# Rotating the MLA queries on GpSimd alone, spreading the w_up sums over 18 items, and moving the low-rank scaling and the key rotation back

## The chip, the cores and the metric

The kernel runs on one core of a Trainium2 chip. The metric is the time of one execution in microseconds (us). TensorE is written PE (its weight loads PEld), VectorE DVE, ScalarE ACT, GpSimd POOL; SP is the engine whose queue issues most of the transfers.

## The reference, cut to what matters

The program is a two-layer encoder trunk on 1024 tokens of width 1024, in float32. Each layer has a mixer with three head groups, a cross-attention to 256 memory tokens, and a gated feed-forward network. The change touches the mixer's latent attention (MLA) and one preparation of the feed-forward network. What is computed there:

```python
qa = (rms_norm(c_q, mla_q_norm) @ mla_w_uq).reshape(B, S, 6, 64 + 32)
q_nope, q_pe = qa[..., :64], apply_rope(qa[..., 64:], *rope_a)
kva = (rms_norm(c_kv, mla_kv_norm) @ mla_w_ukv).reshape(B, S, 6, 64 + 64)
k_pe = apply_rope(k_rope.reshape(B, S, 1, 32), *rope_a)    # one key part for all six heads

def apply_rope(x, cos, sin):                               # pairs (a, b) of neighbouring elements
    return a * cos - b * sin, a * sin + b * cos
```

Six GQA heads stand beside the six MLA heads. Each head's scores are a 1024 x 1024 matrix, its softmax is taken by rows, and the result multiplies the values.

## The kernel before

Float32 operands are split into a high and a low part of a type that PE multiplies fast: `split` (L121 to L127) lets ACT write the high part and DVE the low one (lines L123 and L124, or L126 and L127 with a scale), and `mm3` (L116 to L118) makes a product from three matmuls. Weights go through `load`: a transfer, a high part by ACT (L108) or POOL (L110), and a low part by DVE (L111).

The mixer first multiplies the normalised input by the columns of `w_in` in stages; the last stage gives the low-rank query `cq` (two tiles, one for each half of the tokens), the low-rank key and value `ckv`, and the 32 rotary key columns `kr`. At the last token tile of each half, the code computes the root mean squares (L551 and L552 on DVE, a power on POOL in L553) and scales `cq` and `ckv` on DVE (L556, two instructions). After the stage `rope` rotates `kr`: four products and two sums, of which POOL makes two products (L237, L239) and DVE the rest (L236, L238, L240, L241).

Then `attention` runs 24 items, one for each head and half of the queries: items 0 to 11 are GQA, 12 to 23 MLA. An item has four steps of 128 query rows. A step multiplies queries and keys into a pair of PSUM banks (L726 and L727 for GQA, `mm3` for MLA); DVE finds the row maximum (L295), ACT the exponential with its sum (L299), DVE the reciprocal (L304), and POOL scales the row (L305). PE transposes the scaled rows (L140), which needs all four steps of the item, and multiplies them by the values (L318, L319); POOL adds the two halves of the result (L328). The four steps of an item are called scale 0 to scale 3 below, by their L305; scale 3 is the one that the transposes wait for last.

Between these steps stands other work, taken from `fill[i]`, the list of functions of item i: the transposes of `cq` and the up-projection of the queries (`turn_cq`, `q_cols`) in items 0 to 3, the rotation of each MLA head's queries (`rope_q(h)` in item 8 + 2h, with the same `rope`), the sum of squares of the outputs (L664), and more. `extra[i]` holds the transfers of item i. They prepare block sums of the weight `w_up`: 24 times `copy` copies a piece in DRAM by a transfer of SP (L778), and `add` adds another piece to it by an accumulating transfer that POOL issues (L783); an add waits until its copy has landed. Steps n = 0 to 23 are copied in item n * 14 // 24 and added four items later. The same list holds 12 copies for `w_down`, over 20 items.

Tiles are taken from 46 slots. A scheduler orders the instructions of each engine when the program is built, by its own estimate of when each is ready, so instructions can stand earlier in an engine's order than in the code; each engine then works in that order.

Of the kernel before, what the change touches and what calls it, by code (L numbers as in the profile page):

```python
# [8 lines left out]
F32 = mybir.dt.float32  # L9
F32R = mybir.dt.float32r  # L10
AF = mybir.ActivationFunctionType
ALU = mybir.AluOpType
AX = mybir.AxisListType

P = 128
D = 1024
S = 1024
NT = S // P
KT = D // P
CH = 512  # L20
NC = S // CH
TPC = CH // P
DEPTH = 2
EPS = 1e-6
GRID_W = 64
ROPE_THETA = 10000.0
MLA_H, NOPE, ROPE, QK_A = 6, 64, 32, 96
# [42 lines left out]
def trunk(ctx: ExitStack, tc: tile.TileContext, a: dict, out: bass.AP):  # L70
    nc = tc.nc
# [7 lines left out]
    sl = Slots(spool, SLOTS)  # L79
# [7 lines left out]
    def stat():  # L87
        return stats.tile([P, 16], F32, tag="stat", name="stat")
# [7 lines left out]
    def v3(ap, b):  # L96
        return ap.rearrange("p (a b) -> p a b", b=b)
# [134 lines left out]
    def rope(z, cos, sin, tmp):  # L232

        ev, od = z[..., 0], z[..., 1]
        t0, t1, t2, t3 = tmp
        nc.vector.tensor_tensor(t0, ev, cos, ALU.mult)  # L236
        nc.gpsimd.tensor_tensor(t1, od, sin, ALU.mult)  # L237
        nc.vector.tensor_tensor(t2, ev, sin, ALU.mult)  # L238
        nc.gpsimd.tensor_tensor(t3, od, cos, ALU.mult)  # L239
        nc.vector.tensor_tensor(ev, t0, t1, ALU.subtract)  # L240
        nc.vector.tensor_tensor(od, t2, t3, ALU.add)  # L241
# [142 lines left out]
    def layer(l, nt, w_m, last):  # L384
# [129 lines left out]
        def turn_q(j, c):  # L514
# [7 lines left out]
            if c == 1:  # L522
                sl.put(zq[j])

        cq = [sl.get(F32) for _ in range(2)]
        ckv = sl.get(F32)
        kr = lpool.tile([P, NT * ROPE], F32, tag="kr", name="kr")
        for t in range(NT):
# [17 lines left out]
            if t == 6:  # L546
                turn_q(0, 0)
                turn_q(0, 1)
            if tt == TPC - 1:
                v, r = stat(), stat()  # L550
                nc.vector.tensor_scalar(v[:, 0:4], ssq[:, 0:4], 1.0 / 256, EPS, ALU.mult, ALU.add)  # L551
                nc.vector.tensor_scalar(v[:, 4:8], ssq[:, 4:8], 1.0 / P, EPS, ALU.mult, ALU.add)  # L552
                nc.gpsimd.tensor_tensor(r[:, :8], v[:, :8], mhalf[:, :8], ALU.pow)  # L553
                for z, n, o in ((cq[c], 256, 0), (ckv[:, c * CH : (c + 1) * CH], P, 4)):
                    z = v3(z, n)
                    nc.vector.tensor_tensor(z, z, r[:, o : o + 4].unsqueeze(2).to_broadcast([P, TPC, n]), ALU.mult)  # L556
        put2(w_a)
# [3 lines left out]
        cos3, sin3 = v3(tab[:, T_COSA : T_COSA + P], 16), v3(tab[:, T_SINA : T_SINA + P], 16)  # L561
        tmp = sl.get(F32)
        rope(kr.rearrange("p (t i two) -> p t i two", i=16, two=2), cos3, sin3, [v3(tmp[:, o * P : (o + 1) * P], 16) for o in range(4)])
        sl.put(tmp)

# [41 lines left out]

        def rope_q(h):
            tmp = sl.get(F32)
            z = v3(qn[h][:, : NT * QK_A], QK_A)[:, :, NOPE:]  # L610
            rope(z.rearrange("p t (i two) -> p t i two", two=2), cos3, sin3, [v3(tmp[:, o * P : (o + 1) * P], 16) for o in range(4)])
            sl.put(tmp)
            if h == MLA_H - 1:
                sl.put(tab)

# [183 lines left out]
        items += [mla(h, c) for h in range(MLA_H) for c in range(NC)]  # L799
        fill[0] += [lambda k=k: turn_cq(0, k) for k in range(2)]  # L800
        fill[1] += [lambda k=k: turn_cq(1, k) for k in range(2)]
# [7 lines left out]
        for h in range(MLA_H):  # L809
            fill[8 + 2 * h] += [lambda h=h: rope_q(h)]  # L810
        fill[7] += [lambda c=c: turn_kr(c) for c in range(NC)]
# [40 lines left out]
        for n, (w, m, i) in enumerate(steps):  # L852
            g = n * 14 // len(steps)
            extra.setdefault(g, []).append(lambda w=w, m=m, i=i: w.copy(m, i))
            extra.setdefault(g + 4, []).append(lambda w=w, m=m, i=i: w.add(m, i))
        later = deque(sorted(w_d.steps(), key=lambda s: (5, 7, 6, 3).index(s[1])))
# [626 lines left out]
```

## Time and profile before

| | us |
|---|---|
| median of 3 runs | 2800.31 (2798.71 to 2804.17) |
| the profiled execution | 2792.72 |
| its span, first to last instruction | 2790.7 |
| PE busy in it | 2732.1 (98%) |
| DVE busy | 1966.8 (70%) |
| ACT busy | 1469.7 (53%) |
| POOL busy | 688.0 (25%) |

Where a row ends in square brackets, the number is the time for which the engine stood idle before that instruction, and behind the arrow stands what ended this idle time by the profile. A wait for several things is put down to the one that came last; a wait for a transfer can be shown with another name. PEclk is the TensorE clock that was granted, as a share of full speed.

### The profile page before, as it was taken

To read this page: it belongs to the slowest core of one execution; us is meant where nothing else is said; L and a number is where in the kernel's file an instruction comes from. 1 tells how busy PE (TensorE), PEld (TensorE's weight loads), DVE (VectorE), ACT (ScalarE), POOL (GpSimd) and SP (SyncE) were. 2 spreads that over 40 slices of the span, in tenths; PEclk is the share of its full clock that TensorE was granted. 3 is DMA by queue.
4 is the path that set the end of the run, shared out by engine and by line. 5 is a ranking of instruction groups with operands and counts; after the bars stand their busy time and mean duration, and the time that the engine had idled before them with its cause. 6 is when DMAs were issued, how large, how long until landed. Compare 5 with 4: busy or idle time off the path is not lost.

```text
span 2790.7 us, 37974 instructions
## 1 busy us (share of the span) xinstructions
PE 2732.1 (98%) x13648; PEld 2289.4 (82%) x13648; DVE 1966.8 (70%) x2953; ACT 1469.7 (53%) x2838; POOL 688.0 (25%) x696
## 2 busy tenths in 40 slices
PE   9999999999999999999999999999999999999998
PEld 7987778888878888888889877788888788888887
DVE  5489889666697777774445798895566877777754
ACT  4368878324564444553333788782245544446442
POOL 3245666320001100000123355653200011100000
PEclk9999999999999999999999999999999999999999
DMA  4028991221149876785210389912211698757752
GB/s 145 27 80 229 264 243 38 79 65 48 65 138 237 227 211 169 223 270 185 86 59 21 108 244 251 226 39 68 69 61 46 165 242 221 205 173 233 257 184 104
DMA packets 160748, 418.80 MB, mean 150 GB/s; under 512 B 17840, under 2 KB 18480, under 8 KB 146224
## 3 DMA queue, kind: packets, MB, share of 16 engines
q1 hardware_dynamic: 137376, 323.84, 34.3%
q0 software_dynamic: 23040, 92.28, 18.1%
q8 instruction: 107, 1.75, 0.2%
q14 instruction: 81, 0.66, 0.1%
q10 hardware_dynamic: 144, 0.26, 0.0%
HBM read 371.75 MB, written 206.05 MB: 207 GB/s over the span
## 4 chain that ended last, share of the span: by engine, by line
PE 84%; DVE 6%; ACT 4%; issue 2%; POOL 2%; DMA 1%; SPq 0%; POOLq 0%; DVEq 0%; ACTq 0%
PE bank L1237 8%; PE bank L116 7%; PE bank L118 7%; PE bank L117 7%; PE pair L1237 6%; PE bank L140 6%; PE bank L1125 5%; PE bank L1126 5%; PE bank L1124 5%; PE pair L1124 4%; PE pair L1125 4%; PE pair L1126 4%; PE pair L116 2%; PE pair L118 2%; PE pair L117 2%; PE bank L319 2%
## 5 line engine op out<-in xcount | busy, mean ns | idle before, releaser
L116 PE MATMUL bank<-s,s 128*128 128x512 f32 (+4 forms) x1124 | 405.1, 360 | 5.6 <-DVE s L124 3.8
L124 DVE TENSOR_TENSOR s<-bank,s 128x512 fp32r<-128x512 f32 (+3 forms) x552 | 330.8, 630 | 106.1 <-ACT s L123 103.4
L118 PE MATMUL bank<-s,s 128*128 128x512 f32 (+4 forms) x1124 | 400.0, 357 | 5.4 <-DVE s L127 4.2
L117 PE MATMUL bank<-s,s 128*128 128x512 f32 (+4 forms) x1124 | 399.0, 355 | 0.3 <-DVE s L111 0.3
L123 ACT ACTIVATE s<-bank 128x512 fp32r<-128x512 f32 (+3 forms) x552 | 286.3, 556 | 208.9 <-PE bank L140 138.0
L140 PE MATMUL bank<-ident,s 128*128 128x128 f32 (+1 forms) x2320 | 327.8, 275 | 22.8 <-ACT s L327 6.4
L140 PEld LDWEIGHTS bank<-ident,s 128*128 128x128 f32 (+1 forms) x2320 | 272.4, 140 | 84.2 <-ACT s L327 12.2
L1077 ACT ACTIVATE s<-s 128x512 fp32r<-128x512 f32 x308 | 187.4, 627 | 181.5 <-PE bank L1126 46.6
L305 POOL TENSOR_SCALAR s<-s,stat 128x1024 f32<-128x1024 f32 x192 | 224.5, 1176 | 217.1 <-DVE stat L304 152.9
L1125 PE MATMUL bank<-s,s 128*128 128x512 f32 x704 | 274.5, 390 | 0.9 <-DVE s L209 0.9
L1126 PE MATMUL bank<-s,s 128*128 128x512 f32 x704 | 273.9, 389 | 0.0
L1124 PE MATMUL bank<-s,s 128*128 128x512 f32 x704 | 273.8, 389 | 0.0
L295 DVE TENSOR_REDUCE stat<-pair 128x1 f32<-128x1024 f32 x192 | 233.8, 1218 | 45.9 <-PE pair L727 27.1
L1237 PE MATMUL bank<-s,s 128*128 128x512 f32 (+1 forms) x1068 | 242.6, 387 | 1.6 <-DVE stat L131 1.6
L116 PEld LDWEIGHTS bank<-s,s 128*128 128x128 f32 x1124 | 212.4, 189 | 33.9 <-DVE s L124 5.6
L132 POOL TENSOR_TENSOR stat<-stat,mhalf 128x1 f32<-128x1 f32 (+3 forms) x94 | 82.2, 875 | 634.7 <-DVE stat L131 633.1
L118 PEld LDWEIGHTS bank<-s,s 128*128 128x128 f32 x1124 | 212.3, 189 | 31.1 <-DVE s L127 5.1
L1222 DVE TENSOR_TENSOR s<-s,s 128x512 fp32r<-128x512 f32 x264 | 170.8, 686 | 93.5 <-ACT s L1221 93.5
L1237 PEld LDWEIGHTS bank<-s,s 128*128 128x128 f32 x1068 | 198.7, 188 | 42.3 <-DVE x L1328 1.8
L117 PEld LDWEIGHTS bank<-s,s 128*128 128x128 f32 x1124 | 212.6, 189 | 23.8 <-DVE s L111 0.6
L299 ACT ACTIVATE s<-pair,stat 128x1024 f32<-128x1024 f32 x192 | 214.9, 1119 | 26.1 <-DVE stat L295 22.1
L1221 ACT ACTIVATE s<-s 128x512 fp32r<-128x512 f32 x264 | 153.7, 623 | 141.8 <-DMA s<-g_u 49.6
(182 smaller groups left out, 5529.2 us busy)
## 6 DMA issues: line engine op xcount, KB each, us to landing
s<-u SPq DMA_DIRECT2D x176, 256.0 KB, 4.2
u<-in_w_up SPq DMA_DIRECT2D x40, 1024.0 KB, 17.9
s<-in_w_up SPq DMA_DIRECT2D x132, 256.0 KB, 4.4
g_u<-s SPq DMA_DIRECT2D x88, 256.0 KB, 2.8
s<-g_u SPq DMA_DIRECT2D x88, 256.0 KB, 3.2
s<-d SPq DMA_DIRECT2D x88, 256.0 KB, 3.5
u<-in_w_up POOLq DMA_DIRECT2D x20, 1024.0 KB, 21.1
u<-u POOLq DMA_DIRECT2D x20, 1024.0 KB, 15.9
```

Of the source, the lines that this page charges most:

```text
L116: nc.tensor.matmul(o, l[0], r[0], start=first, stop=False)
L117: nc.tensor.matmul(o, l[0], r[1], start=False, stop=False)
L118: nc.tensor.matmul(o, l[1], r[0], start=False, stop=last)
L123: nc.scalar.activation(hi, src, AF.Copy)
L124: nc.vector.tensor_tensor(lo, src, f(hi), ALU.subtract)
L140: nc.tensor.transpose(b[:m, j * P : (j + 1) * P], s, ident)
L295: nc.vector.reduce_max(self.nm[:, 0:1], s, axis=AX.X, negate=True)
L305: Item.last = nc.gpsimd.tensor_scalar(p, p, r[:, 0:1], 0.0, ALU.mult, ALU.add)
L1124: nc.tensor.matmul(o, lh, rh, start=k == 0 and m in (1, 5, 6), stop=False, skip_group_check=True)
L1125: nc.tensor.matmul(o, lh, rl, start=False, stop=False, skip_group_check=True)
L1126: nc.tensor.matmul(o, ll, rh, start=False, stop=k == 3, skip_group_check=True)
L1237: nc.tensor.matmul(o, lh[p], rh[q], start=m in (1, 5, 2) and i == 0 and k == 0, stop=i == NP - 1 and k == 2, skip_group_check=True)
```

## The change

The scaling of the low-rank parts becomes a function `norm_low`; for the first half of the tokens it is called where it stood, for the second half it becomes a piece of `fill[0]`, behind `turn_cq(0, k)`. The rotation of `kr` becomes a piece of `fill[4]` and is otherwise the same. `rope_q` makes all four products and both sums on POOL, in two pieces (three instructions each) of `fill[8 + 2h]`. The 24 steps of `w_up` are copied in item n * 18 // 24 and added three items later.

```diff
+        def norm_low(c, ssq):
+            v, r = stat(), stat()
+            nc.vector.tensor_scalar(v[:, 0:4], ssq[:, 0:4], 1.0 / 256, EPS, ALU.mult, ALU.add)
+            nc.vector.tensor_scalar(v[:, 4:8], ssq[:, 4:8], 1.0 / P, EPS, ALU.mult, ALU.add)
+            nc.gpsimd.tensor_tensor(r[:, :8], v[:, :8], mhalf[:, :8], ALU.pow)
+            for z, n, o in ((cq[c], 256, 0), (ckv[:, c * CH : (c + 1) * CH], P, 4)):
+                z = v3(z, n)
+                nc.vector.tensor_tensor(z, z, r[:, o : o + 4].unsqueeze(2).to_broadcast([P, TPC, n]), ALU.mult)
...
-            if tt == TPC - 1:
...
+            if t == TPC - 1:
+                norm_low(0, ssq)
...
-        tmp = sl.get(F32)
-        rope(kr.rearrange("p (t i two) -> p t i two", i=16, two=2), cos3, sin3, [v3(tmp[:, o * P : (o + 1) * P], 16) for o in range(4)])
-        sl.put(tmp)
+
+        def rope_k():
+            tmp = sl.get(F32)
+            rope(kr.rearrange("p (t i two) -> p t i two", i=16, two=2), cos3, sin3, [v3(tmp[:, o * P : (o + 1) * P], 16) for o in range(4)])
+            sl.put(tmp)
...
-        def rope_q(h):
...
+        def rope_q(h, half):
+
+            z = v3(qn[h][:, : NT * QK_A], QK_A)[:, :, NOPE:].rearrange("p t (i two) -> p t i two", two=2)
+            ev, od, tt = z[..., 0], z[..., 1], nc.gpsimd.tensor_tensor
+            if half == 0:
+                rtmp[h] = sl.get(F32)
+            t0, t1, t2, t3 = (v3(rtmp[h][:, o * P : (o + 1) * P], 16) for o in range(4))
+            if half == 0:
+                tt(t0, ev, cos3, ALU.mult)
+                tt(t1, od, sin3, ALU.mult)
+                tt(t2, ev, sin3, ALU.mult)
+            else:
+                tt(t3, od, cos3, ALU.mult)
+                tt(ev, t0, t1, ALU.subtract)
+                tt(od, t2, t3, ALU.add)
...
-        fill[0] += [lambda k=k: turn_cq(0, k) for k in range(2)]
+        fill[0] += [lambda k=k: turn_cq(0, k) for k in range(2)] + [lambda: norm_low(1, ssq)]
+        fill[4] += [rope_k]
...
-            fill[8 + 2 * h] += [lambda h=h: rope_q(h)]
+            fill[8 + 2 * h] += [lambda h=h, i=i: rope_q(h, i) for i in range(2)]
...
-            g = n * 14 // len(steps)
+            g = n * 18 // len(steps)
...
-            extra.setdefault(g + 4, []).append(lambda w=w, m=m, i=i: w.add(m, i))
+            extra.setdefault(g + 3, []).append(lambda w=w, m=m, i=i: w.add(m, i))
```

Where the scheduler put these instructions is shown at three places. The first is DVE at the start of the first layer's attention. Before, the row maximum of the first step (L295) is followed by the scaling (L556), the rotation of `kr` (L236 to L241), the low part of the second weight tile (L111) and, among them, the low parts of the transposed `cq` (L127):

```order
L111 TENSOR_TENSOR s_131_1612<-s_129_1610,s_130_1611 128x768
L551 TENSOR_SCALAR stat<-stat 128x4
L552 TENSOR_SCALAR stat<-stat 128x4
L295 TENSOR_REDUCE stat<-pair 128x1
L556 TENSOR_TENSOR s_102_1255<-s_102_1255,stat 128x1024
L556 TENSOR_TENSOR s_103_1256<-s_103_1256,stat 128x512
L236 TENSOR_TENSOR s_132_1616<-kr,s_73_703 128x128
L111 TENSOR_TENSOR s_128_1606<-s_126_1604,s_127_1605 128x576
L238 TENSOR_TENSOR s_132_1616<-kr,s_73_703 128x128
L127 SCALAR_TENSOR_TENSOR s_135_1670<-bank,cols_86,s_134_1669 128x512
L240 TENSOR_TENSOR kr<-s_132_1616 128x128
L241 TENSOR_TENSOR kr<-s_132_1616 128x128
```

The same place after the change, where L527, L528 and L532 are the new lines of L551, L552 and L556:

```order
L111 TENSOR_TENSOR s_131_1605<-s_129_1603,s_130_1604 128x768
L295 TENSOR_REDUCE stat<-pair 128x1
L127 SCALAR_TENSOR_TENSOR s_134_1656<-bank,cols_86,s_133_1655 128x512
L127 SCALAR_TENSOR_TENSOR s_136_1665<-bank,cols_86,s_135_1664 128x512
L527 TENSOR_SCALAR stat<-stat 128x4
L528 TENSOR_SCALAR stat<-stat 128x4
L295 TENSOR_REDUCE stat<-pair 128x1
L111 TENSOR_TENSOR s_128_1599<-s_126_1597,s_127_1598 128x576
L532 TENSOR_TENSOR s_102_1255<-s_102_1255,stat 128x1024
L532 TENSOR_TENSOR s_103_1256<-s_103_1256,stat 128x512
```

The two L127 now stand right behind the first L295, the scaling behind the second, and the rotation of `kr` is gone from here.

The second place is POOL at the rotation of MLA head 3. Before, scale 1 (s_334), two adds, scale 2 (s_340), a sum of squares (L664), scale 3 (s_343), and then the two products of the rotation:

```order
L305 TENSOR_SCALAR s_334_3837<-s_334_3837,stat 128x1024
L783 DMA u_5_4_1627<-in_w_up 128x2048
L783 DMA u_5_5_1628<-in_w_up 128x2048
L305 TENSOR_SCALAR s_340_3884<-s_340_3884,stat 128x1024
L664 TENSOR_TENSOR s_318_3683<-s_318_3683,s_344_3936 128x1024
L305 TENSOR_SCALAR s_343_3930<-s_343_3930,stat 128x1024
L237 TENSOR_TENSOR s_348_3974<-s_142_1712,s_73_703 128x128
L239 TENSOR_TENSOR s_348_3974<-s_142_1712,s_73_703 128x128
L305 TENSOR_SCALAR s_347_3968<-s_347_3968,stat 128x1024
```

After the change the same stretch reads so (L682 is the new line of L664, L801 that of L783, L621 to L627 are the rotation):

```order
L305 TENSOR_SCALAR s_334_3830<-s_334_3830,stat 128x1024
L801 DMA u_3_2_1629<-u_6_2_1617 128x2048
L305 TENSOR_SCALAR s_340_3877<-s_340_3877,stat 128x1024
L682 TENSOR_TENSOR s_318_3676<-s_318_3676,s_344_3928 128x1024
L621 TENSOR_TENSOR s_348_3966<-s_141_1705,s_73_703 128x128
L622 TENSOR_TENSOR s_348_3966<-s_141_1705,s_73_703 128x128
L623 TENSOR_TENSOR s_348_3966<-s_141_1705,s_73_703 128x128
L625 TENSOR_TENSOR s_348_3966<-s_141_1705,s_73_703 128x128
L626 TENSOR_TENSOR s_141_1705<-s_348_3966 128x8x16
L305 TENSOR_SCALAR s_343_3922<-s_343_3922,stat 128x1024
L627 TENSOR_TENSOR s_141_1705<-s_348_3966 128x8x16
L305 TENSOR_SCALAR s_347_3960<-s_347_3960,stat 128x1024
```

Five of the six instructions of the rotation now stand ahead of scale 3, and one add stands there in place of two. Of the other heads only head 2 has a part of its rotation (three instructions) ahead of a scale 3; at heads 1, 4 and 5 they stand behind it, and at head 0 they stand, all six in a row, ahead of a scale 2.

The third place is POOL about an item after the last rotation. Before, between scale 2 (s_403) and scale 3 (s_406) stood a power (L132) and three products of the gated group's scaling (L711), and no add was left behind them:

```order
L305 TENSOR_SCALAR s_403_4568<-s_403_4568,stat 128x1024
L132 TENSOR_TENSOR stat<-stat,mhalf 128x4
L711 TENSOR_TENSOR s_78_941<-s_78_941,stat 128x512
L711 TENSOR_TENSOR s_79_952<-s_79_952,stat 128x512
L711 TENSOR_TENSOR s_78_941<-s_78_941,stat 128x512
L305 TENSOR_SCALAR s_406_4609<-s_406_4609,stat 128x1024
L711 TENSOR_TENSOR s_79_952<-s_79_952,stat 128x512
```

After the change (L729 is the new line of L711) most of the scaling stands behind scale 3, with adds between:

```order
L305 TENSOR_SCALAR s_403_4563<-s_403_4563,stat 128x1024
L132 TENSOR_TENSOR stat<-stat,mhalf 128x4
L729 TENSOR_TENSOR s_78_941<-s_78_941,stat 128x512
L801 DMA u_6_5_1620<-u_5_5_1614 128x2048
L305 TENSOR_SCALAR s_406_4605<-s_406_4605,stat 128x1024
L305 TENSOR_SCALAR s_409_4645<-s_409_4645,stat 128x1024
L801 DMA u_7_5_1626<-in_w_up 128x2048
L328 TENSOR_TENSOR s_414_4692<-s_415_4693 64x512
L729 TENSOR_TENSOR s_78_941<-s_78_941,stat 128x512
```

One L729 and one add are left ahead of scale 3 there. Outside the two attention stretches no engine's order differs.

## Rows read from the trace of the kernel before

**Rows 1.** The page's busy times: us, share of the span, instructions.

```profile
PE 2732.1 (98%) x13648; PEld 2289.4 (82%) x13648; DVE 1966.8 (70%) x2953; ACT 1469.7 (53%) x2838; POOL 688.0 (25%) x696
```

**Rows 2.** Busy time by engine in the two attention stretches; then PEclk, DMA share, GB/s.

```profile
165.00:530.00 365.00, 348.48 (x1978) 287.11 (x1977) 313.24 (x518) 286.70 (x593) 202.51 (x190) 1.00 0.64 170
1547.50:1912.50 365.00, 348.94 (x1966) 287.48 (x1965) 309.91 (x515) 286.28 (x592) 202.75 (x190) 0.99 0.63 168
```

**Rows 3.** Timeline at the start of attention, layer one: start, duration, engine, line.

```profile
167.74 2.35 DVE L556 TENSOR_TENSOR s<-s,stat 128x1024 f32<-128x1024 f32 x2 [0.49 <-POOL stat L553]
171.09 0.74 DVE L127 SCALAR_TENSOR_TENSOR s<-bank,cols,s 128x512 fp32r<-128x512 f32 x1
168.61 0.69 ACT L108 ACTIVATE s<-s 128x576 fp32r<-128x576 f32 x1
171.88 0.40 PE L118 MATMUL bank<-s,s 128*128 128x288 f32 x1 [2.11 <-DVE s L127]
```

**Rows 4.** Windows with a lowered clock, columns as in Rows 2.

```profile
307.00:309.30 2.30, 2.30 (x7) 1.65 (x7) 1.57 (x2) 2.29 (x5) 0.83 (x2) 0.50 1.03 246
1556.20:1559.60 3.40, 3.40 (x16) 3.40 (x16) 2.40 (x4) 2.64 (x13) 1.16 (x2) 0.51 0.00 0
1750.66:1755.00 4.34, 4.34 (x16) 3.61 (x17) 2.54 (x5) 3.13 (x7) 3.10 (x3) 0.61 1.01 268
```

**Rows 5.** DVE's first product of the query rotations: ns min/median/max, first and last start.

```profile
L236 DVE TENSOR_TENSOR s<-s,s x12: 274/926/5337, 272.3 to 1795.3; 128x128 f32<-128x128 f32 x12
```

**Rows 6.** Timeline at the rotation of head 3, layer two.

```profile
1741.13 0.84 POOL L783 DMA_DIRECT2D u<-in_w_up  x1 [4.17 <-DVE stat L304]
1741.69 1.43 POOL L305 TENSOR_SCALAR s<-s,stat 128x1024 f32<-128x1024 f32 x1
1742.22 5.34 DVE L236 TENSOR_TENSOR s<-s,s 128x128 f32<-128x128 f32 x1
1742.78 2.69 POOL L664 TENSOR_TENSOR s<-s,s 128x1024 f32<-128x1024 f32 x1
1745.17 1.39 POOL L305 TENSOR_SCALAR s<-s,stat 128x1024 f32<-128x1024 f32 x1
1746.61 0.44 PE L140 MATMUL bank<-ident,s 128*128 128x128 f32 x2 [1.26 <-POOL s L305]
1750.66 0.98 PE L140 MATMUL bank<-ident,s 128*128 128x128 f32 x4 [2.92 <-ACT s L327]
```

**Rows 7.** PE's timeline behind the rotations of heads 1, 3 and 5, layer one.

```profile
305.78 0.50 PE L319 MATMUL bank<-s,s 128*128 128x512 f32 x1 [2.13 <-DVE s L124]
366.55 0.66 PE L140 MATMUL bank<-ident,s 128*128 128x128 f32 x4 [2.66 <-ACT s L327]
412.16 0.63 PE L140 MATMUL bank<-ident,s 128*128 128x128 f32 x4 [0.97 <-DVE s L124]
```

**Rows 8.** PE's timeline behind the scaling of the gated group, layer one.

```profile
424.35 0.44 PE L140 MATMUL bank<-ident,s 128*128 128x128 f32 x2 [1.00 <-POOL s L305]
```

**Rows 9.** POOL's product in the query rotations: ns min/median/max.

```profile
L237 POOL TENSOR_TENSOR s<-s,s x12: 470/505/732, 270.2 to 1796.2; 128x128 f32<-128x128 f32 x12
```

**Rows 10.** POOL's and PE's timeline at the rotations of heads 2 and 3, layer one.

```profile
330.87 1.12 POOL L305 TENSOR_SCALAR s<-s,stat 128x1024 f32<-128x1024 f32 x1 [1.52 <-PE bank L319]
361.06 1.38 POOL L305 TENSOR_SCALAR s<-s,stat 128x1024 f32<-128x1024 f32 x1
362.81 0.38 PE L140 MATMUL bank<-ident,s 128*128 128x128 f32 x2
```

**Rows 11.** Transfers from 235 to 420 us: window row, two queues, copies' median to landing.

```profile
235.00:420.00 185.00, 174.17 (x974) 140.72 (x973) 159.97 (x278) 151.64 (x308) 111.31 (x108) 0.99 1.01 254
...
q0 software_dynamic: 3346, 22.30, 62.3%
q1 hardware_dynamic: 3490, 24.53, 37.9%
...
u<-in_w_up SPq DMA_DIRECT2D x15, 1024.0 KB, 23.6
```

More of the change, by code (lines that the diff above doesn't have):

```diff
@@ L548, in layer @@
                 turn_q(0, 1)
-            if tt == TPC - 1:
[L550 to L556, printed above, removed]
+            if t == TPC - 1:
+                norm_low(0, ssq)
         put2(w_a)
@@ L606, in v_cols @@
                 split(v3(b[:, j * P : (j + 1) * P], 64), d[:, :, :64], d[:, :, 64:])
-        def rope_q(h):
[L609 to L614, printed above, removed]
+        def rope_q(h, half):
[12 more added lines that the diff above has]
+                tt(od, t2, t3, ALU.add)
+                sl.put(rtmp[h])
+                if h == MLA_H - 1:
+                    sl.put(tab)
+        rtmp = {}
         def copy_kr(j):
```

## The prediction

> **What bounds the kernel now.** I read the busy times first: PE is busy 98% of the span, so the end is set by PE, and a change can win only what PE still loses [rows 1]. The busy times of the attention stretches come next, since only there does any engine's order change. The reader is to see that PE is busy 348.48 and 348.94 of 365 us: it loses 16.5 and 16.1 us, 32.6 together, while DVE works 313 us of 365 and is the next fullest engine [rows 2]. That is the ceiling of any gain in waits. Then I asked in the timeline of PE for every wait inside these stretches and what stood on the engine that ended it.
>
> At the start of attention PE stands 2.11 us for a low part that DVE writes (L127), and as long in layer two [rows 3]. DVE had it late because the scaling (L556, from 167.74 us) and part of the key rotation run first; the L127 starts at 171.09.
>
> Behind the query rotations there are three more places in layer one: 2.13 us at head 1, 2.66 at head 3 and 0.97 at head 5 [rows 7]. In layer two head 3 costs 1.26 and 2.92 [rows 6], head 5 again 0.97 (same pattern), head 1 only 0.3. Behind each of the large ones stands one DVE instruction, L236, which takes 274 ns at its shortest and 5337 at its longest, for the same 128 x 128 elements [rows 5]. Rows 6 show why: it began at 1742.22, while POOL worked through a chain without a gap (a scale, L664 at 1742.78, a scale at 1745.17, two products of the rotation), and ended when that chain did. Meanwhile DVE found no row maximum, ACT no exponential, and PE ran dry. The chain was without a gap because POOL had stood 4.17 us before at an add (L783); the row names DVE, but a reciprocal cannot hold an add, and the transfers are full there, so I read it as the copy that had not landed.
>
> Behind three of these waits PE runs on at a granted clock of about 0.5 of 2.4 GHz, its lower level of 1.2 GHz: the windows give 2.30 us at 0.50, 3.40 at 0.51, 4.34 at 0.61 [rows 4], a loss of 2.30 x 0.50 + 3.40 x 0.49 + 4.34 x 0.39 = 4.5 us. The same 2.11 in layer one and the 2.66 were followed by no fall.
>
> **The change part by part.** *Scaling and key rotation moved back.* The two L127 now stand right behind the first row maximum, that is about where L556 began, 3.35 us sooner than 171.09 [rows 3]. PE stopped at 171.88 - 2.11 = 169.77, so it no longer stops for them. What is late next is the second weight tile: ACT ends its high part at 168.61 + 0.69 = 169.30 [rows 3] and DVE's low part follows, so a few tenths stay. Gain 2 x 1.8 = 3.6 (2.6 to 4.2). The moved scaling is still two DVE instructions, 2.35 us, behind the second row maximum now; what hides them is that the next scores wait for a free pair anyway.
>
> The key rotation comes back in item 4 with its four DVE instructions, so it can meet the same chain on POOL. Bounds: nothing, as at heads 0, 2 and 4, or the 4.18 of head 3. No add stands shortly ahead of it, so I take the near end, 0.2 in each layer: -0.4 (0 to -8.4).
>
> *Query rotations on POOL alone.* L236 and its three companions leave DVE 12 times. With them go the waits that they cause: 2.13 + 2.66 + 1.26 + 2.92 + 2 x 0.97 = 10.9 us [rows 6, 7]. The Trainium skill ("SBUF — State Buffer", section "Who interferes with whom") says that a DVE instruction with two SBUF inputs and a GpSimd one that reads SBUF exclude each other, and that the second blocks until the first has finished. The trace agrees that it blocks, but not how long: L664 and the next scale started after L236 and still went first [rows 6]. By the rule a stall ends with one POOL instruction, at most 0.9 us here, and the gain would be nearer 6 x 0.9 = 5.4 than 10.9; the measurement decides.
>
> POOL gets four more instructions per head. One takes 505 ns [rows 9], so 2.0 us per head, 24 in all. Where they stand behind scale 3 they cost nothing: the scale next in line is used one to three steps later, and a step is 365 / 25.25 / 4 = 3.6 us. Two heads are left. At head 2 three products, 1.5 us, stand ahead of scale 3, where POOL stood idle 1.52 [rows 10]: 0 to 1.5, I take 0.3. At head 3 five, 2.5 us. There scale 3 ended at 361.06 + 1.38 = 362.44 and PE turned its rows at 362.81 without a wait [rows 10], so 0.4 is spare, and up to 2 us come free if the add ahead no longer holds POOL: 0 to 2.1, I take 1.0. Both layers: -2.6 (0 to -7.3). If the cover of the other four heads is gone, 2.0 each, see below.
>
> The Trainium skill ("GPSIMD Engine Reference", section "4.1 Engine selection") speaks against this edit: elementwise work with two inputs belongs on VectorE, GpSimd being about twice as slow. The rows agree on the ratio, 505 to 274 ns; by that rule the 24 us would be the bill, and the first rival is what it would do here.
>
> *Sums over 18 items.* From 235 to 420 us the transfers are full, 1.01 [rows 11]. POOL's queue took 62.3% of 185 us for 22.30 MB, 5.17 us per MB, SP's 37.9% for 24.53 MB, 2.86 per MB. One layer has 23.07 MB to copy and to add, and 11.53 MB for `w_down` over 20 items. Before, an item had 1.65 MB: 8.5 + 4.7 + 1.65 = 14.9 us of transfers in the 14.5 of an item, so a backlog grew. After, 1.28 MB: 6.6 + 3.7 + 1.65 = 12.0, a share of 0.82. A copy took 23.6 us in the median [rows 11]; with three items, 43.5 us, to the add, it has landed. I give this no gain of its own; it is what keeps the head 3 price small. Four or so adds come into items 18 to 20. There PE waits 1.00 us in each layer for a scale behind the gated scaling [rows 8]; one product and one add are now ahead of that scale in place of three products. Gain 1.0 (0 to 2.0).
>
> *Clock.* With its waits the falls can go: 4.5 at most. Others may come, so I take 3.0 (0 to 4.5).
>
> **Sum:** 3.6 - 0.4 + 10.9 - 2.6 + 1.0 + 3.0 = 15.5 us. From the profiled execution's 2792.72 that gives 2777.2. The median of the runs, 2800.31, lies 7.6 above that execution; with the same distance the forecast is 2784.8. All ends together give 21.6 us, and some of the 15 us of other PE waits may go with a freer DVE, so 2775; with the poor ends and no clock, about 3 to 7, so 2795. The likeliest case's own range is 2776 to 2794.
>
> **The rivals.** *POOL's scales become the wait.* The scheduler set its order from its own estimates, so the slack at heads 0, 1, 4 and 5 may not be there on the chip. For it: POOL is full around the adds and PE already waits for a scale 1.26 and 1.00 us [rows 6, 8]. Against it: POOL is busy 203 of 365 us [rows 2] and scale 3 stands ahead at four of six heads. At half price, 12 us in place of 2.6, the gain is 6: 2794. At full price, 24, it is slower by 6: 2806.
>
> *Only the start is on the path.* The pile-up comes from the add; if POOL still stands at adds, PE waits for scale 3 where it waited for DVE, and 3.6 plus half of the clock is left, about 5: 2795. For it: 1.26 of head 3's 4.18 was already a wait for POOL. Against it: three times as much was DVE's.
>
> *The shorter lead* (slower). An add now follows its copy by three items, not four. Place: L783, with the scales queued behind it on POOL. If transfers stay full, a copy lands as late as before and POOL stands up to an item, 14.5 us, longer at each of the three places where it stood two us or more: 43 us, less 18 gained, 2826. It decides once the share stays at 1.0; the 0.82 above speaks against it.
>
> **How the numbers follow.** Forecast 0.70, POOL's scales 0.15, only the start 0.10, the lead 0.05. The measurement can tell about 0.2%, 5.6 us, from no change, a limit at 2794.7 and 2805.9. The forecast lies below it almost wholly; of POOL's scales about half, of the second rival a little under half do. So faster 0.80, within 0.13, slower 0.07. The range reaches to both middle rivals: 2775 to 2798.
>
> **What would show it.** L621 to L627 near 0.5 us each and no DVE instruction of 128 x 128 over 1 us, save perhaps the key rotation; no PE wait over 1 us behind heads 1, 3 and 5; the wait of 2.11 at the start under 0.8; DMA share near 0.8 from 235 to 420 us and no POOL idle over 1 us ahead of an add. PE's loss in each stretch would fall from 16 us to 8 or 10. It is wrong if PE waits for L305 add up to more than 5 us a layer, or if adds still hold POOL for several us.

## The result and the profile after

The changed kernel takes 2770.46 us in the median of four runs (2770.12 to 2771.39); the kernel before took 2799.84 beside it (2798.71 to 2804.17). The ratio is 0.9894, interval 0.9879 to 0.9909: 29 us faster, where 15.5 were forecast. The time lies below the range.

The page's busy times of the changed kernel (columns as in [rows 1]), then busy time by engine in its two attention stretches [rows 2]:

```profile
PE 2724.2 (98%) x13648; PEld 2284.4 (83%) x13648; DVE 1941.6 (70%) x2905; ACT 1470.8 (53%) x2838; POOL 706.3 (26%) x744
```

```profile
165.00:530.00 365.00, 355.72 (x2021) 293.82 (x2019) 304.78 (x500) 290.50 (x597) 217.70 (x218) 1.00 0.65 174
1543.00:1908.00 365.00, 356.72 (x2018) 295.07 (x2017) 301.83 (x495) 287.51 (x589) 217.42 (x219) 1.00 0.65 173
```

The reader is to see that PE now loses 9.3 and 8.3 us of 365, in place of 16.5 and 16.1, and that POOL is busier by 15 us a stretch; PE pays for that at head 3 alone, shown below.

The start of attention in the changed kernel, DVE and PE, answers to [rows 3]:

```profile
165.14 1.22 DVE L295 TENSOR_REDUCE stat<-pair 128x1 f32<-128x1024 f32 x1
166.28 1.40 DVE L127 SCALAR_TENSOR_TENSOR s<-bank,cols,s 128x512 fp32r<-128x512 f32 x2
167.08 0.54 PE L118 MATMUL bank<-s,s 128*128 128x288 f32 x2
```

Both low parts are there at 167.68, and no row of PE has a wait behind them. The wait of 2.11 is gone in both layers.

The rotation's first and last instruction, ns min/median/max (to [rows 5, 9]), and the transfers from 235 to 420 us (to [rows 11]):

```profile
L621 POOL TENSOR_TENSOR s<-s,s x12: 453/462/708, 268.3 to 1774.7; 128x128 f32<-128x128 f32 x12
L627 POOL TENSOR_TENSOR s<-s x12: 446/464/676, 270.4 to 1776.8; 128x128 f32<-128x128 f32 x12
```

```profile
235.00:420.00 185.00, 178.05 (x1010) 145.68 (x1009) 155.29 (x266) 158.29 (x320) 125.33 (x136) 1.00 0.92 239
...
q0 software_dynamic: 2691, 18.13, 50.9%
q1 hardware_dynamic: 3755, 25.97, 40.4%
...
u<-in_w_up SPq DMA_DIRECT2D x17, 1024.0 KB, 14.0
```

The share fell from 1.01 to 0.92, not to the 0.82 of the prediction: the price per MB is as it was (5.2 and 2.9 us), but 44.1 MB were moved in these 185 us, where the prediction's rate gives 40. The copies' median to landing fell from 23.6 to 14.0 us. No add (L801) of the two stretches has an idle time ahead of it; before, six had (3.87, 0.32, 2.44, 1.90, 1.08 and 4.17 us), together 13.8 us. No DVE product of 128 x 128 elements takes over 0.6 us any more.

Head 3, layer one, POOL and PE (to [rows 6, 7, 10]):

```profile
346.63 1.12 POOL L305 TENSOR_SCALAR s<-s,stat 128x1024 f32<-128x1024 f32 x1 [2.26 <-DVE stat L304]
347.74 2.39 POOL L682 TENSOR_TENSOR s<-s,s 128x1024 f32<-128x1024 f32 x1
350.10 0.46 POOL L621 TENSOR_TENSOR s<-s,s 128x128 f32<-128x128 f32 x1
...
352.21 1.11 POOL L305 TENSOR_SCALAR s<-s,stat 128x1024 f32<-128x1024 f32 x1
...
353.38 0.76 PE L140 MATMUL bank<-ident,s 128*128 128x128 f32 x5 [2.50 <-POOL s L305]
```

DVE gave the reciprocal for scale 3 at 348.85. POOL came to it at 352.21, behind L682 and five instructions of the rotation, so PE stood 2.50 us; layer two shows 2.50 as well. This is the longest wait that is left. The others over 1 us are 1.41 and 1.39 behind head 5, where an exponential (L299) stands on ACT behind three high parts of splits (L123); the 1.00 of [rows 8] is gone:

```profile
418.55 0.50 PE L116 MATMUL pair<-s,s 96*128 96x512 f32 x1 [1.41 <-ACT s L299]
```

Of the lowered clock in attention [rows 4] one stretch is left, behind head 3 in layer two:

```profile
1727.40:1730.90 3.50, 3.50 (x12) 2.92 (x13) 1.38 (x2) 2.94 (x6) 1.43 (x2) 0.53 1.01 246
```

### The profile page after: what moved, and what is told of

It is laid out like the page before. It is cut to its first block, busy times and chain, and to the rows that moved or that the text cites. A ratio compares the mean times of both kernels' runs of the same rounds, so it can differ in the third digit from the quotient of the medians.

```text
span 2768.8 us, 37951 instructions
## 1 busy us (share of the span) xinstructions
PE 2724.2 (98%) x13648; PEld 2284.4 (83%) x13648; DVE 1941.6 (70%) x2905; ACT 1470.8 (53%) x2838; POOL 706.3 (26%) x744
## 4 chain that ended last, share of the span: by engine, by line
PE 85%; DVE 5%; ACT 3%; DMA 3%; POOL 2%; issue 1%; SPq 0%; POOLq 0%; DVEq 0%; ACTq 0%
PE bank L1256 8%; PE bank L116 7%; PE bank L118 7%; PE bank L117 7%; PE bank L140 7%; PE pair L1256 6%; PE bank L1144 5%; PE bank L1145 5%; PE bank L1143 5%; PE pair L1143 4%; PE pair L1144 4%; PE pair L1145 4%; PE bank L318 3%; PE bank L319 3%; PE pair L116 2%; PE pair L118 2%
## 5 line engine op out<-in xcount | busy, mean ns | idle before, releaser
L123 ACT ACTIVATE s<-bank 128x512 fp32r<-128x512 f32 (+3 forms) x552 | 286.0, 556 | 205.7 <-PE bank L140 142.5
L295 DVE TENSOR_REDUCE stat<-pair 128x1 f32<-128x1024 f32 x192 | 233.5, 1216 | 39.6 <-PE pair L118 19.0
L132 POOL TENSOR_TENSOR stat<-stat,mhalf 128x1 f32<-128x1 f32 (+3 forms) x94 | 84.3, 897 | 634.3 <-DVE stat L131 634.1
L1241 DVE TENSOR_TENSOR s<-s,s 128x512 fp32r<-128x512 f32 x264 | 170.6, 685 | 93.1 <-ACT s L1240 93.1
L1097 DVE TENSOR_TENSOR s<-s,s 128x512 fp32r<-128x512 f32 x308 | 201.7, 686 | 36.2 <-ACT s L1096 33.9
## 6 DMA issues: line engine op xcount, KB each, us to landing
u<-in_w_up POOLq DMA_DIRECT2D x20, 1024.0 KB, 18.4
```

Source lines behind the costliest of these rows:

```text
L123: nc.scalar.activation(hi, src, AF.Copy)
L295: nc.vector.reduce_max(self.nm[:, 0:1], s, axis=AX.X, negate=True)
```

## The experiments

All times are medians; each ratio is to the kernel before on the same chip, with its interval (medians of before there: 2800.06 beside e1 to e4, 2796.45 beside e5 to e8, 2797.54 beside e9 to e12, 2798.45 beside e13 to e15). A ratio can differ from the quotient of the two medians by up to 0.001, so a difference is given by the times and by the ratios where they disagree. Four numbers are read from each trace, which is one execution, both layers added: POOL's idle time ahead of adds, and, from the first row maximum (L295) to the last, PE's waits over 0.15 us, the clock's loss (stretch times one minus the granted share), and the length of that stretch, called attention.

| kernel | time | ratio | adds hold POOL | PE waits | clock | attention |
|---|---|---|---|---|---|---|
| before, profile shown | 2799.84 | 1 | 13.8 | 30.0 | 6.8 | 674.0 |
| before again (e1) | 2801.57 | 1.0002 [0.9993, 1.0011] | 18.4 | 32.2 | 11.9 | 681.5 |
| start only (e2) | 2793.17 | 0.9974 [0.9962, 0.9985] | 17.8 | 28.3 | 6.8 | 672.3 |
| rotation only (e3) | 2789.67 | 0.9965 [0.9952, 0.9979] | 30.5 | 27.4 | 0 | 666.1 |
| sums only (e4) | 2783.47 | 0.9940 [0.9928, 0.9952] | 0 | 22.6 | 3.4 | 662.5 |
| start + sums (e5) | 2773.01 | 0.9921 [0.9907, 0.9934] | 0 | 13.6 | 1.7 | 651.1 |
| start + rotation (e6) | 2776.62 | 0.9929 [0.9917, 0.9942] | 16.7 | 20.0 | 0 | 657.7 |
| before, lead five (e7) | 2779.21 | 0.9934 [0.9922, 0.9947] | 11.7 | 20.5 | 5.1 | 660.1 |
| before, 18 items, lead four (e8) | 2776.07 | 0.9928 [0.9915, 0.9942] | 0.9 | 18.5 | 3.4 | 655.9 |
| changed | 2770.46 | 0.9894 [0.9879, 0.9909] | 0 | 16.6 | 1.7 | 651.5 |
| changed again (e9) | 2772.30 | 0.9916 [0.9904, 0.9929] | 0 | 17.0 | 3.4 | 654.0 |
| changed, lead four (e10) | 2764.42 | 0.9886 [0.9873, 0.9900] | 0 | 11.6 | 1.7 | 647.8 |
| start, 18 items, lead four (e11) | 2761.96 | 0.9882 [0.9866, 0.9898] | 0.2 | 7.8 | 1.7 | 642.8 |
| changed, head 3 later (e12) | 2766.74 | 0.9891 [0.9878, 0.9905] | 0 | 13.0 | 0 | 648.6 |
| rotation + sums (e13) | 2780.61 | 0.9934 [0.9921, 0.9948] | 0 | 22.8 | 6.8 | 661.1 |
| before, rotation on DVE (e14) | 2793.36 | 0.9984 [0.9975, 0.9994] | 20.1 | 29.1 | 6.8 | 672.6 |
| changed, lead four, rotation on DVE (e15) | 2764.99 | 0.9883 [0.9869, 0.9896] | 0 | 10.5 | 1.7 | 647.0 |

Attention less waits less clock lies between 631 and 639 us in every row, so waits and clock are most of what the variants differ in. The rest is not nothing: it is 637 in both profiles of before and 633 to 634 in both of the changed kernel, and what these 4 us are is open. The span outside attention stays within 4 us in all rows.

**The kernel before, once more (e1).** No edit.

> The kernel before, unchanged, profiled once more. Its profiled execution took 2792.72 us and its other runs 2798.7 to 2804.2; the changed kernel's four runs all lie within 1.3 us. Theory V (the kernel before varies from run to run, because the lock-outs of L236 and the falls of the clock come in some runs more than in others): the new profile is taken at another time than 2792.7, near 2800 us, and its trace has longer waits of PE behind the rotations and more stretches with a lowered clock, together some 7 us more than the old one. Rival D (a fixed distance between a profiled execution and the others): the new profile is again near 2793 us and the runs near 2800.

The profile was taken at 2801.57 us: theory V. Against the profile of before that execution lost 2.2 us more in waits and 5.1 more in clock, 7.3 of the 7.5 us by which its attention is longer; the spans differ by 8.9. So most of the difference is the clock. POOL's adds and DVE's first product at head 3, layers one and two:

```profile
359.91 0.82 POOL L783 DMA_DIRECT2D u<-in_w_up  x1 [4.14 <-DVE stat L295]
361.04 5.29 DVE L236 TENSOR_TENSOR s<-s,s 128x128 f32<-128x128 f32 x1
...
1746.91 0.84 POOL L783 DMA_DIRECT2D u<-in_w_up  x1 [4.53 <-DVE stat L304]
1747.64 5.70 DVE L236 TENSOR_TENSOR s<-s,s 128x128 f32<-128x128 f32 x1
```

The same place of layer one in the profile of before:

```profile
357.02 0.81 POOL L783 DMA_DIRECT2D u<-in_w_up  x1 [2.44 <-DVE s L124]
359.83 3.60 DVE L236 TENSOR_TENSOR s<-s,s 128x128 f32<-128x128 f32 x1
362.57 0.71 POOL L239 TENSOR_TENSOR s<-s,s 128x128 f32<-128x128 f32 x1
```

With 4.17 and 5.34 of [rows 6] these are four pairs: 2.44 and 3.60, 4.14 and 5.29, 4.17 and 5.34, 4.53 and 5.70. The product takes 1.15 to 1.17 us more than POOL stood at the add, each time, and so in e2 (4.00 and 5.17, 3.47 and 4.64). It ends 6.41 to 6.43 us after the add begins, just behind the last POOL instruction of the chain (L239 ends at 363.28 here, the product at 363.43), whenever it started. What the add costs, DVE's product pays a little later.

Over all 56 runs of before in these comparisons the time goes from 2791.69 to 2806.42, and only one is at or under the 2792.72 of the profile on which the forecast was built. Each run comes with its mean granted clock: of the 52 runs beside e1 to e15, the three at 0.993 took 2802.87 to 2806.42, the eight at 0.996 took 2791.69 to 2798.81. So the spread of the kernel before goes with the clock.

**Each part alone (e2, e3, e4).** The edits are the three parts of the change, each put into the kernel before by itself.

> The kernel before with the scaling of the second half and the key rotation moved back only; the query rotations and the w_up sums stay as before. Theory S (each part takes away its own waits): the start's waits of 2.11 + 0.42 + 0.28 us go in each layer, 5 us, and 1.7 us of lowered clock in layer two, so 5 to 7 us faster than before, near 2794; the waits behind the rotations of heads 1, 3 and 5 stay. Rival K (the moved key rotation meets POOL's adds and is locked out as L236 was): L236 of the key rotation takes over 1 us and the gain is under 3 us, 2797 or more.

> The kernel before with the query rotations on POOL alone, in two pieces; the start and the w_up sums stay as before. Theory S (each part takes away its own waits): the 10.9 us of waits behind the rotations go, and some 5 us of lowered clock, less 2.1 us a layer where five products stand ahead of head 3's scale 3: 10 to 13 us faster, 2787 to 2790. Rival A (the adds make the pile-ups): POOL still stands at the adds (L783) for several us and PE now waits for L305 where it waited for DVE; the gain is under 4 us, 2796 or more.

> The kernel before with the w_up steps over 18 items and the add three items behind the copy only. Theory S (each part takes away its own waits): the sums alone give little; L236 still meets POOL chains without a gap, and only the waits for adds shrink: 0 to 4 us faster, 2796 to 2800. Rival A (the adds make the pile-ups): with a copy landed before its add POOL has no backlog, L236's largest duration falls under 1.5 us, and most of the 10.9 us of waits and of the lowered clock go: 12 to 18 us faster, 2782 to 2788.

The start gives 7 us, as its own waits say, and the moved key rotation meets nothing (its L236 takes 0.33 us). The rotation gives 10, inside theory S, though rival A's sign is there: POOL stands 30.5 us at adds and PE waits for scale 3. In its trace PE's waits are hardly shorter (27.4 us for 30.0); what is gone is the clock's loss (0 for 6.8). The add and the wait at head 3, layer one, of the rotation-only kernel:

```profile
356.56 0.82 POOL L796 DMA_DIRECT2D u<-in_w_up  x1 [6.05 <-DVE s L124]
...
362.03 0.44 PE L140 MATMUL bank<-ident,s 128*128 128x128 f32 x2 [1.60 <-POOL s L305]
```

The sums alone give 17 us, the most of the three, as rival A had it. With the rotation left on both engines, DVE's first product (ns min/median/max) is short already, though its longest, 1.67 us, is a little over the 1.5 that rival A gave:

```profile
L236 DVE TENSOR_TENSOR s<-s,s x12: 276/346/1673, 273.0 to 1785.1; 128x128 f32<-128x128 f32 x12
```

**Two parts of three (e5, e6, e13).** The changed kernel with one part undone.

> The changed kernel with the query rotations as before (products and sums on DVE and POOL); start and w_up sums as changed. So far the parts alone gave about 7 us (start), 10 us (rotation) and 17 us (sums), 34 together, and the whole change 29. Theory A (the adds that hold POOL are the common cause; the sums remove it, and the rotation is then worth little more): L236 stays under 2 us, no add holds POOL, and the time is near 2800 - 7 - 17 = 2776, so the rotation's own share in the change is about 5 us. Rival S (the rotation takes away waits of its own): 2780 or more, the rotation still worth 10.

> The changed kernel with the w_up steps over 14 items and the add four items behind the copy, as before; start and rotation as changed. Theory A (the adds that hold POOL are the common cause): POOL still stands some 15 us a layer at adds, runs of this kernel vary by several us again, and the time is near 2800 - 7 - 10 = 2783, so the sums' share in the change is 12 us or more. Rival S (the sums only kept head 3's price small): 2772 to 2776, the sums worth under 5 us.

> The changed kernel with the start of attention as before (the scaling of the second half and the key rotation in their old places); rotation and sums as changed. Theory B (the start is worth more beside the other two than alone, since behind it PE has no other large waits that take the gain back): 8 to 11 us slower than the changed kernel, near 2780. Rival F (the start is worth what its own waits say, 2.11 + 0.42 + 0.28 us a layer and 1.7 us of clock): 5 to 7 us slower, near 2777.

Without the rotation (e5) attention takes 651.1 us, with it 651.5 and 654.0 (e9): in the traces it is worth nothing beside the other two parts. The ratios leave it 1 to 8 us (0.9921, beside 0.9916 of e9 and 0.9894); theory A had said 5, rival S 10. The waits of 2.13, 2.66, 2.92 and 0.97 are gone in e5 as well, since L236 is short. At head 3 PE still waits 1.49 and 1.51 us there for scale 3, which stands on POOL behind the sum of squares and the old rotation's two products. The product, then the wait:

```profile
L236 DVE TENSOR_TENSOR s<-s,s x12: 274/282/346, 273.9 to 1774.2; 128x128 f32<-128x128 f32 x12
...
354.46 0.44 PE L140 MATMUL bank<-ident,s 128*128 128x128 f32 x2 [1.49 <-POOL s L305]
```

Without the sums (e6) both theories missed: the sums are worth 6 us there by the times, 4 to 10 by the ratios. Without the start (e13) the kernel is 8 to 10 us slower by the times, as theory B said; by the ratios it is 5 to 11, which does not rule rival F out. The 2.11 us wait is back in both layers, a fall of the clock behind it, and a wait of 1.1 near 230 us.

```profile
171.53 0.40 PE L118 MATMUL bank<-s,s 128*128 128x288 f32 x1 [2.11 <-DVE s L127]
```

**Rate and lead (e7, e8).** One number each in the kernel before:

```diff
-            extra.setdefault(g + 4, []).append(lambda w=w, m=m, i=i: w.add(m, i))
+            extra.setdefault(g + 5, []).append(lambda w=w, m=m, i=i: w.add(m, i))    # e7
...
-            g = n * 14 // len(steps)
+            g = n * 18 // len(steps)                                                # e8
```

> The kernel before with one number changed: the add follows its copy by five items and not four; the rate stays at 24 steps in 14 items. Theory L (what holds POOL is only that a copy of some 24 us or more has not landed, and a longer lead hides it): the waits ahead of L783 fall under 1 us each, L236's largest duration under 2 us, and 10 to 15 us go, 2785 to 2790. Rival R (the rate is the cause: transfers share is at 1.0 and the backlog grows past any lead of this size): POOL still stands several us ahead of adds, and the time is 2794 to 2800.

> The kernel before with the w_up steps over 18 items and the add four items behind the copy, so the rate alone is changed. Theory R (the rate is the cause): as fast as with three items of lead, 2782 to 2785 beside the 2783.5 of the sums alone, no add holds POOL. Rival L (the position of the adds is what counts: with three items of lead they stand elsewhere among the scales): over 3 us away from 2783.5, in either direction, with POOL's adds elsewhere in its order.

The longer lead is faster than either theory had it: it leaves the transfers nearly full and 11.7 us of hold, and yet gives 17 us. The adds stand elsewhere among the scales, and that is what the trace shows to count. At head 1 of layer one the held add now comes at 310.32, behind the rotation, and the product takes 0.28 us. DVE's first product is long at head 3 alone, 4.05 and 3.48 us in the two layers, where a held add still stands just ahead of it:

```profile
299.74 0.28 DVE L236 TENSOR_TENSOR s<-s,s 128x128 f32<-128x128 f32 x1
310.32 0.81 POOL L783 DMA_DIRECT2D u<-in_w_up  x1 [1.85 <-issue]
...
351.34 0.82 POOL L783 DMA_DIRECT2D u<-u  x1 [2.76 <-DVE s L124]
351.77 4.05 DVE L236 TENSOR_TENSOR s<-s,s 128x128 f32<-128x128 f32 x1
```

So the holds added up do not price a kernel; where each stands does. How much of the 17 us comes of this was not tried by itself. The lower rate with a lead of four (e8) holds no add over 1 us, as theory R said, but is faster than with three, by 7 us in the times and 3 by the ratios: rival L's position, or the copies' 10.1 us to landing in place of 13.8. The rows are, of e7 and then of e8, the window, and the copies' median to landing (last number):

```profile
235.00:420.00 185.00, 179.06 (x1005) 146.56 (x1004) 163.12 (x286) 155.44 (x316) 116.01 (x114) 0.99 0.98 251
...
u<-in_w_up SPq DMA_DIRECT2D x15, 1024.0 KB, 20.8
```

```profile
235.00:420.00 185.00, 180.05 (x1016) 148.13 (x1014) 161.47 (x288) 156.60 (x318) 114.02 (x111) 0.99 0.91 236
...
u<-in_w_up SPq DMA_DIRECT2D x17, 1024.0 KB, 10.1
```

So of the two numbers that the change sets for the sums, the 18 helps, and the 3 in place of 4 costs (e9 against e10 on one chip, 2772.30 to 2764.42, though e10 also moves head 3's rotation behind scale 3, see below; e4 against e8, 0.9940 to 0.9928, point the same way with intervals that overlap).

**The changed kernel again, and three on the same chip (e9 to e12).** In e10 the add follows by four items; e11 has the start and 18 items with lead four, and the old rotation; e12 moves head 3:

```diff
-            fill[8 + 2 * h] += [lambda h=h, i=i: rope_q(h, i) for i in range(2)]
+            fill[8 + 2 * h + (h == 3)] += [lambda h=h, i=i: rope_q(h, i) for i in range(2)]
```

> The changed kernel, unchanged, beside the other three of this group. Theory V (before varies because adds hold POOL now longer, now shorter; the change took that away): all its runs within 2 us of 2770.5 and no wait ahead of an add again, while the kernel before spreads over 5 us or more. Rival D (chance): it spreads over 5 us as well.

> The changed kernel with the add four items behind the copy and not three (18 items as changed). POOL's six instructions of head 3 then stand behind scale 3 in its order. Theory P (the 2.50 us that PE waits for scale 3 in each layer are the price of the rotation standing ahead of it): that wait falls under 0.6 us and the kernel gains 3 to 5 us over the changed one, 2766 to 2768. Rival Q (PE would wait there for something else next, since DVE and ACT are idle too): under 1.5 us gained, 2769 or more.

> The start and the sums over 18 items with the add four items behind, and the query rotations as before (DVE and POOL). Theory A (once no add holds POOL, the rotation on POOL is worth nothing): within 2 us of the same kernel with the rotations on POOL. Rival S (the rotation keeps a worth of its own): 4 us or more slower than that kernel.

> The changed kernel with the rotation of head 3 alone taken from item 14 to item 15; on POOL it then no longer follows L682 and stands, six in a row, between scales 2 and 3 of the next item. Theory P (the 2.50 us wait is POOL's, L682 and five products in one chain): the wait falls to about 0.5 in each layer, 4 us gained, 2766 to 2768. Rival Q (the wait moves with the rotation to the next scale 3): under 1.5 us gained, 2769 or more.

The changed kernel spreads over 4.1 us in five runs (2771.49 to 2775.56), the kernel before beside it over 8.2 in nine: no add waits again, but the spread lies between theory V and rival D. Other variants do not tie the spread to the holds either: e11 (0.2 us of hold) spreads over 7.4 in four runs, e13 (none) over 7.8 in five, e6 (16.7) over 3.0 in five. In e12 the wait of 2.50 is gone, the clock does not fall, and it is 5.6 us faster than e9: theory P. In e10 the wait is gone too, and 7.9 us are gained, more than the 3 to 5 of theory P. In e11 the old rotation is no slower than the new one, 2761.96 to 2764.42 with runs that overlap, and DVE's product is never over half a microsecond:

```profile
L236 DVE TENSOR_TENSOR s<-s,s x12: 273/305/494, 271.6 to 1765.2; 128x128 f32<-128x128 f32 x12
```

e11 beats both kernels: 0.9882 (0.9866 to 0.9898) of before, 10 us under the changed one on its chip.

**The rotation on DVE alone (e14, e15).** `tt` is `nc.vector.tensor_tensor`, in the kernel before with the new `rope_q` (e14) and in e10 (e15).

> The kernel before, its adds and start untouched, with all six instructions of each query rotation on DVE and none on POOL. Theory A (an add holds POOL, its scales and the sum of squares then run without a gap, and a DVE product with two SBUF inputs waits until that chain ends): the first DVE product at head 3 still takes 3 us or more, and the time is within 4 us of before, 2794 to 2802. Rival O (it is the rotation's own two POOL products that keep DVE out): no DVE instruction of 128 x 128 takes over 1.2 us, and 8 us or more go, under 2791.

> The changed kernel with the add four items behind the copy and all six instructions of each query rotation on DVE in place of POOL. Theory A (once no add holds POOL, it matters little which engine rotates): first product under 0.6 us, 2760 to 2766. Rival O (DVE is kept out by POOL's chains whatever the adds do, so POOL is the better place): DVE products of over 1.5 us and 2770 or more.

With adds that hold POOL, DVE's first product still takes 4.06 us at head 3 of layer two, though no query rotation is left on POOL; in layer one the product started while POOL stood at the add, and took 0.28. Layer one, then layer two:

```profile
355.46 0.28 DVE L616 TENSOR_TENSOR s<-s,s 128x128 f32<-128x128 f32 x1
355.81 0.81 POOL L796 DMA_DIRECT2D u<-in_w_up  x1 [5.60 <-DVE s L124]
...
1738.60 0.84 POOL L796 DMA_DIRECT2D u<-in_w_up  x1 [3.71 <-DVE s L124]
1740.14 4.06 DVE L616 TENSOR_TENSOR s<-s,s 128x128 f32<-128x128 f32 x1
```

So DVE is kept out by the burst on POOL behind the hold, and not by the rotation's own products. The time, 2793.36, is just under theory A's 2794 to 2802. With no add holding POOL (e15) DVE rotates as cheaply as POOL does, 2764.99 beside 2764.42 on another chip.

## Why the prediction was wrong

The direction, the bound on PE, and the places were right. The size failed in four steps. Between the two profiled executions the time fell by 22.1 us (2792.72 to 2770.64), where 15.5 were forecast. Attention is 22.5 us shorter: 13.4 are waits (12.5 in the sum), 5.1 the clock (3.0 in the sum), and 4 are in neither, which the sum did not have and which stay open. The other 7 of the 29 us are the distance to the median.

**The distance carried over.** The step "with the same distance the forecast is 2784.8" added 7.6 us, as if a profiled execution were always that much shorter. It was a low execution out of a spread: e1 profiled the same kernel at 2801.57 and showed the rest as more falls of the clock, and longer holds and waits. Where the changed kernel's profile falls in its own spread is another draw: 2770.64 beside a median of 2770.46. Without this step the forecast is 2777.2, inside the range and 6.7 from the measured time.

**The sums.** "I give this no gain of its own; it is what keeps the head 3 price small." By themselves they are the largest part: 17 us of before (e4), and 4 to 10 of the changed kernel (e6). The prediction had read the cause in the trace (the chain "was without a gap because POOL had stood 4.17 us before at an add"), and then booked the 10.9 us to the edit that takes DVE's product away. e5 and e11 keep that product and the waits are gone all the same; e14 keeps the holds and has the long product without a rotation on POOL. The waits of that term did go, and the sums alone remove the large ones (e4 keeps 1.5 us at head 3 and 1.15 behind head 0 in each layer). The new rotation removes the long product too (e3, e6), but while adds hold POOL it puts waits for scale 3 in its place. e7 adds that the held add has to stand just ahead of the rotation. Of the rivals, the shorter lead did not bite (no add waits), but its direction was right: three items are worse than four (e8, e10).

**Head 3.** 1.0 a layer was forecast between 0 and 2.1; PE waits 2.50 there. With no hold ahead POOL is not ahead either: scale 2 and L682 come when they are ready, and L682 and the five instructions stand between a ready scale 3 and PE. Even the old rotation, with the sum of squares and two products ahead of scale 3, leaves a wait of 1.5 a layer (e5). e12 prices it at 5.6 us for both layers, clock included, over the 2.0 of the sum and over its upper end of 4.2.

**Start and clock.** 3.6 was forecast for the start: all of the 2.11 + 0.42 + 0.28 us went in each layer, 5.6 together, since the weight tile that I held to be late next was not; with the clock behind it and a later wait the start is worth 7 alone (e2) and 8 to 10 in the whole (e13). The clock had 6.8 us to give in the profile of before, not 4.5: a stretch from 1780 to 1786 us had been passed over, since no wait stands ahead of it (columns as in [rows 4]):

```profile
1780.00:1786.00 6.00, 6.00 (x25) 4.85 (x25) 3.91 (x8) 3.78 (x7) 3.94 (x3) 0.72 1.05 251
```

In the changed kernel's profile 5.1 of it came back, 3.0 were forecast.

The scaling of the gated group gave its 1.00, and a new wait of 1.4 behind head 5 took it back; it is in e10, e12, e13 and e15, and not in e5 and e11, so it goes with the new `rope_q` beside 18 items, on whichever engine.

Two sums of the prediction do not come out as written: the poor ends without a gain in the clock add up to -2.2, not to 3 to 7, and the transfers of the changed kernel filled 0.92 of the time, not 0.82. Neither bears on the miss: the time came out below the range, and no add waited.

What was put down to the Trainium skill ("SBUF — State Buffer", section "Who interferes with whom"), that the second of two instructions blocks until the first has finished, stays as [rows 6] had it: the block lasts longer than one instruction, and in e1 to the end of POOL's burst. That it is the access to SBUF which keeps DVE out is read from the rows, not shown: no run took that access alone away.

## What to carry to other kernels

An engine that stands at a transfer pays again afterwards: its queued work runs as one burst, and whoever shares something with it waits for the whole burst, so look for the hold before the burst and remove it, or move it to where nothing meets the burst. Where several edits could remove the same wait, book the gain to the cause, and try each alone. A profile is one draw from the runs: where the kernel's times spread, see where yours stands in them, and do not carry its distance from the median over to another kernel.

## What the runs showed of the hardware

- A DVE product of 128 x 128 elements with two inputs in SBUF took 0.27 to 5.70 us. At head 3 of both profiles of before and of e2 it took POOL's hold at the add plus 1.15 to 1.17, in six cases of six; in each of them POOL instructions that began after it went first, as they followed without a gap.
- The granted clock's falls cost about 1.7 us each, and the traces' sums are multiples of it (1.7, 3.4, 5.1, 6.8): PE runs on for 3.5 us at about 0.5 of 2.4 GHz, its 1.2 GHz level. Behind the same 2.1 us wait it fell in some executions and not in others, and once it fell with no wait over 0.15 us in the 11 us before (at 1781 us in the profile of before); what decides is open.
- The same transfers, asked for over 18 items in place of 14 with a lead of four, landed in 10.1 us in the median (e8) in place of 23.6.
